# Norm boundaries of a two-layer encoder: sample tiles handled in pairs, another order on VectorE, two weight units split ahead

## The chip, the cores and the metric

The kernel runs on one core of one Trainium2 chip. The metric is the time of one execution on the device in microseconds (us). Five engines work side by side, each with its own in-order queue of instructions: TensorE (PE, with its weight loads shown apart as PEld), VectorE (DVE), ScalarE (ACT), GpSimd (POOL) and SyncE (SP), which here only issues transfers. An instruction that waits holds up everything behind it in its queue.

## The reference

Two sequences, a prompt of 512 tokens and a sample of 256 tokens, run through two layers of the same form. D is 1024.

```python
for l in range(DEPTH):                                   # 2 layers
    mod = (silu(c) @ ada_w[l] + ada_b[l]).reshape(B, 9, D)
    h = x * (1 + mod[:, 1]) + mod[:, 0]
    x = layer_norm(ALPHA*x + 0.5*(1 + mod[:, 2]) * swiglu(h, ffn1), ln[l, 0])
    h = x * (1 + mod[:, 4]) + mod[:, 3]
    o = concat(rms(window_attention(h)), rms(hyena(h))) @ w_out[l]
    x = layer_norm(ALPHA*x + (1 + mod[:, 5]) * o, ln[l, 1])
    h = x * (1 + mod[:, 7]) + mod[:, 6]
    x = layer_norm(ALPHA*x + 0.5*(1 + mod[:, 8]) * swiglu(h, ffn2), ln[l, 2])
```

There are six parts: feed-forward (FFN), mixer, FFN, and the same again. Between two parts stands a layer norm followed by the modulation of the next part. These five places are called boundaries 1 to 5 here. After boundaries 1 and 4 the next part is a mixer, after 2, 3 and 5 it is an FFN. Boundaries 2 and 5 come out of a mixer.

## The kernel before

Activations lie with features on the partitions: eight feature tiles d = 0 to 7 of 128 features, each with 512 prompt columns and 256 sample columns. Every product is done in three matmuls, since both operands are split in a high part (fp32r) and a low part (the rest): high weight by high activation, high weight by low activation, low weight by high activation (`mm3`). The low part of an activation is made by VectorE as value minus high part (`Norm.low`, L400), and the matmuls that read it wait for it.

Weights come in units of 128x1024 floats. `w_load` (L236) lets SP bring a unit into one of seven buffers slot_r; `w_ahead` (L243) then splits it into a buffer slot_w: ScalarE copies the high part, VectorE subtracts for the low part, and then the next load is asked for. `w_take` hands out split units in order. So a weight unit is ready when both engines have got to its split in their queues.

A boundary is written in `final` (L547). First `sample_out` makes the last product of the sample. Then a loop over d makes the prompt's last product (18 matmuls of 512 columns for each d out of an FFN, 12 out of a mixer). In that loop the sample's norm is worked off beside it: `stats` (sums over features by transposes and reductions), `bcast` (TensorE spreads 1/sigma and mean/sigma over the partitions, into two PSUM banks), and `apply` (L385) for two feature tiles per d. One `apply` is: VectorE multiplies by the first bank and subtracts the second (tile t), GpSimd writes the normed x, ScalarE writes the high part of the next h and its full value, and VectorE later subtracts for the low part. The last statement of each turn is `add` (L333): VectorE adds the product to x (scalar_tensor_tensor, called the residual here), ScalarE squares it, GpSimd adds it to the sum S, and VectorE adds the previous square to Q.

Then `Proj.head` (L459) starts the next part. It takes n units (4 before a mixer, 6 before an FFN) and makes for each the sample's product, 24 matmuls of 256 columns, in the order of the units; after unit 0 it calls the prompt's `stats`, and after the third unit `bcast` and eight prompt `apply`. Only then come the prompt's products, first for four units together and feature tile by feature tile, then for units 4 and 5. Before an FFN the full values of feature tiles 4 to 7 are kept in four of the seven slot_r (`Fast.full`, L689), and `Fast.early` (L701) takes two more for a later pair of units, after unit 0.

The order of the work is that of the program text; buffers are handed out by a rehearsal of the program, so that a tile gets the buffer that has been free longest. Each operation is recorded through one helper, L70, so rows below are told apart by tiles: slot_s holds activations, slot_w split weights, slot_r raw weights and full values, slot_t temporaries, bank a PSUM bank.

Of the kernel before, what the change touches and what calls it, by code (L numbers as in the profile page):

```python
# [14 lines left out]
ALU = mybir.AluOpType  # L15
AX = mybir.AxisListType

P = 128
D = 1024
ND = D // P  # L20
# [10 lines left out]
SEQ = (slice(0, LP), slice(LP, T), slice(0, LP // 2), slice(LP // 2, LP))  # L31
SLEN = (LP, LS, LP // 2, LP // 2)
# [45 lines left out]
class _Memory:  # L78
# [32 lines left out]
    def const(self, name, shape, dtype=F32):  # L111
        if not self.real:
            return _View(None)
        return self.pool.tile([P] + shape, dtype, tag=name, name=name)[:]
# [46 lines left out]
def _program(mem, nc, x_in, c_col, c_row, w_units, ada_nat, ada_t, ada_b, ln_p, conv_p, sink_in, grp_in,  # L161
             f_z, f_w1, f_v, f_w23, f_w4, f_decay, f_bias, f_t, dft_k, dft_y, dft_u, rope_in, mask_in, sgn_in, y_out):
    vec, act, gp, pe, sp = (mem.engine(getattr(nc, n) if mem.real else None)
                            for n in ("vector", "scalar", "gpsimd", "tensor", "sync"))
# [4 lines left out]
    def slot_w(shape, dtype=F32R):  # L169
        return mem.alloc("slot_w", shape, dtype)  # L170
# [6 lines left out]
    def slot_t(shape, dtype=F32):  # L177
        return mem.alloc("slot_t", shape, dtype)
# [9 lines left out]
    def f32(ap):  # L188
        return ap.bitcast(F32)

    def tt(out, a, b, op, eng=vec):
        eng.tensor_tensor(out=out, in0=a, in1=b, op=op)

    def ts(out, a, s1, s2=None, op0=ALU.mult, op1=ALU.add, eng=vec):
        if s2 is None:
            eng.tensor_scalar(out=out, in0=a, scalar1=s1, scalar2=None, op0=op0)
        else:
            eng.tensor_scalar(out=out, in0=a, scalar1=s1, scalar2=s2, op0=op0, op1=op1)
# [4 lines left out]
    def acopy(out, a):  # L203
        act.activation(out=out, in_=a, func=AF.Copy)

    def affine(out, a, scale, bias):
        act.activation(out=out, in_=a, func=AF.Identity, scale=scale, bias=bias)
# [11 lines left out]
    lnp = const("lnp", [DEPTH, 3, 2, ND])  # L219
# [12 lines left out]
    n_units = len(w_order)  # L232
    w_raw, w_split = {}, {}
    w_state = {"dma": 0, "split": 0, "next": 0, "limit": w_stops.pop(0), "raws": 3}

    def w_load(upto):  # L236
        while w_state["dma"] < min(upto, w_state["limit"]):
            i = w_state["dma"]
            w_raw[i] = slot_r([D])
            sp.dma_start(w_raw[i], w_units[w_order[i]])  # L240
            w_state["dma"] += 1

    def w_ahead(n):  # L243
        while w_state["split"] < min(w_state["next"] + n, w_state["limit"]):
            i = w_state["split"]
            w_load(i + 1)
            raw = w_raw.pop(i)
            w = slot_w([2, D])
            acopy(w[:, 0], raw)
            tt(w[:, 1], raw, f32(w[:, 0]), ALU.subtract)  # L250
            w_split[i] = w
            w_state["split"] += 1
            w_load(i + w_state["raws"])
# [27 lines left out]
    class Feat:  # L281
# [9 lines left out]
        def __call__(self, d, cols):  # L291
            if d // 4 not in self.t:
                self.more(d // 4)
            return self.t[d // 4][:, d % 4, cols]

    def new_h():
        return Feat(F32R), Feat(F32R)

# [20 lines left out]
    class Norm:  # L319
# [65 lines left out]
        def apply(self, s, d):  # L385

            n, c = SLEN[s], SEQ[s]
            x, t = self.x(d, c), slot_t([n])
            tt(t, x, self.r[s][:, :n], ALU.mult)
            if len(self.waiting) > 1:  # L390
                self.low()
            tt(t, t, self.mr[s][:, :n], ALU.subtract)
            ts(x, t, lnp[:, self.l, self.which, 0, d:d + 1], lnp[:, self.l, self.which, 1, d:d + 1], eng=gp)
            hh, hl, G, B = self.nxt
            v = t if self.full is None else self.full(d, c)
            affine(hh(d, c), t, G[:, d, s:s + 1], B[:, d, s:s + 1])
            affine(v, t, G[:, d, s:s + 1], B[:, d, s:s + 1])
            self.waiting.append((hl(d, c), hh(d, c), v))

        def low(self):  # L400
            if self.waiting:
                lo, hi, t = self.waiting.pop(0)
                tt(lo, t, f32(hi), ALU.subtract)
# [124 lines left out]
    def sample_out(os, norm):  # L528

        for o in os:  # L530
            for i in range(4):
                if i in o.hooks:
                    o.hooks[i]()
                outs = []
                for j in range(2):
                    b, more = o.place(1, 2 * i + j, j == 1)
                    o.d([(b, 1)], 2 * i + j, more=more)
                    outs.append(b)
                for j in range(2):
                    if o is os[-1]:  # L540
                        norm.add(2 * i + j, 1, outs[j])
                    else:
                        norm.plain(2 * i + j, 1, outs[j])
                pump(1)
        drain()

    def final(os, norm, proj, n_head, spill):  # L547

        sample_out(os, norm)
        o = os[-1]  # L550
        n_units = sum(o.n for o in os)
        when = (0, 2, 3) if n_units > 4 else (1, 3, 4)
        for d in range(ND):
            bp, more = o.place(0, d)
            for i, part in enumerate(os):
                part.d([(bp, 0)], d, more=more or i > 0, less=part is not o)
            w_ahead(min(4, 6 - n_units + sum((d + 1) * part.n // 8 for part in os)))
            if d == when[0]:
                norm.stats(1)
            if d == when[1]:  # L560
                norm.bcast(1)
            for i in range(2 * (d - when[2]), 2 * (d - when[2]) + 2):
                if 0 <= i < ND:
                    norm.apply(1, i)
            norm.add(d, 0, bp)
        for i in range(2 * (ND - when[2]), ND):
            norm.apply(1, i)
        for j in range(2):
            spill(1, j)
        norm.low()  # L570
        norm.low()
        norm.squares()
        w_ahead(6)

        def hook(i):
            if i == 0:
                norm.stats(0)
            elif i == 2:
                norm.bcast(0)
                for d in range(ND):  # L580
                    norm.apply(0, d)
                    if d % 4 == 3:
                        spill(0, d // 4)
                norm.low()
                norm.low()
            if i == 0:
                proj.early()

        proj.head(n_head, hook)
# [82 lines left out]
    class Fast:  # L672
# [144 lines left out]
        def late(self):  # L817

            j = self.j
            self.prep_a_high(j)  # L820
            self.prep_a_low(j)
            self.sums(j)
            for low in (self.prep_b(j), self.prep_c(j), self.prep_v3(j)):
                low()
            self.raw.pop(j)
# [302 lines left out]
    x = Feat()  # L1128
# [30 lines left out]
    G, B = modul(0, 0, None)  # L1159
    filt[0].spectra(1, sides(ts1[2], skip, ts1[3], skip, skip, filt[1].flush, skip, skip))  # L1160
    ts1[4]()
    ts1[5]()
    filt[1].flush()
    h = new_h()

    def first_h(d):
# [9 lines left out]
    part = swiglu(x, *h, 0, 0)  # L1176
# [578 lines left out]
    for i in range(len(PARTS)):  # L1755
# [5 lines left out]
        part = part[1](lambda os, xx, coef, i=i: finish(i, os, xx, coef))  # L1761
# [159 lines left out]
```

## Time and profile before

| what | value |
|---|---|
| median of 3 runs | 2927.01 us (2925.14 to 2927.79) |
| profiled execution, its own time | 2925.08 us |
| its span in the trace | 2923.3 us |
| TensorE busy | 2837.8 us (97%) |
| VectorE busy | 2138.7 us (73%) |
| ScalarE busy | 1345.9 us (46%) |
| GpSimd busy | 331.5 us (11%) |
| mean granted TensorE clock | 0.989 of full speed |

The span runs from the first to the last instruction. In rows of the timeline the columns are start, duration, engine, operation with tiles and shape, and in square brackets the idle time of the engine before it with what ended that idle time. A row with "x5" holds five instructions in sequence, and its duration covers all five.

### The profile page before, as it was taken

How to read it: one execution, taken by the hardware profiler on the slowest of the kernel's cores; microseconds unless marked ns; L12 is line 12 of the kernel's file. 1: busy time of each engine (PE TensorE's matmuls, PEld its weight loads, DVE VectorE, ACT ScalarE, POOL GpSimd, SP SyncE). 2: the span in 40 equal slices, each digit the busy share in tenths (PEclk: the TensorE clock that was granted, in tenths of full speed). 3: DMA queues.
4: the chain of work that ended last, by engine and by line, in shares of the span. 5: the costliest groups of instructions: out<-in, count | busy, mean ns of one | idle time of the engine just before them, and what ended most of it. 6: DMA issues, size and time to landing. Idle time of an engine off the chain costs nothing. (4 is left out here: it accounts for less than half of the span.)

```text
span 2923.3 us, 42304 instructions
## 1 busy us (share of the span) xinstructions
PE 2837.8 (97%) x16564; PEld 2599.3 (89%) x16564; DVE 2138.7 (73%) x3797; ACT 1345.9 (46%) x2307; POOL 331.5 (11%) x394
## 2 busy tenths in 40 slices
PE   9999999999999999999999999999999999999998
PEld 3789999988888889999988999998888888999997
DVE  5788778878968887786588777657896787444558
ACT  3544444444366544444445444444436654444444
POOL 2400000021000400000030000002100030000000
PEclk9999999999999999999999999999999999999999
DMA  5546665542121135664333665343312112455432
GB/s 203 194 174 173 189 176 163 145 147 102 68 73 61 55 134 155 194 195 120 107 120 123 180 175 159 104 111 133 107 70 74 60 50 92 82 115 116 99 108 82
DMA packets 102608, 364.67 MB, mean 125 GB/s; under 512 B 13750, under 2 KB 17031, under 8 KB 99208
## 3 DMA queue, kind: packets, MB, share of 16 engines
q1 hardware_dynamic: 74968, 259.88, 24.8%
q0 software_dynamic: 27440, 102.08, 16.3%
q8 instruction: 130, 2.13, 0.3%
q14 instruction: 70, 0.57, 0.1%
HBM read 284.33 MB, written 80.74 MB: 125 GB/s over the span
## 5 line engine op out<-in xcount | busy, mean ns | idle before, releaser
L70 PE MATMUL bank<-slot_s,slot_w 128*128 128x384 f32 (+2 forms) x13176 | 2321.4, 336 | 46.6 <-DVE slot_s L70 27.1
L70 PEld LDWEIGHTS bank<-slot_s,slot_w 128*128 128x128 f32 x13176 | 2129.7, 190 | 215.0 <-DVE slot_s L70 23.3
L70 DVE TENSOR_TENSOR slot_w<-slot_w,slot_w 128x1024 fp32r<-128x1024 f32 (+2 forms) x444 | 369.8, 864 | 4.1 <-ACT slot_w L70 1.6
L70 DVE CUSTOM_DVE_ANT_0 slot_t<-slot_r,slot_r 128x1024 bf16<-128x1024 f32 x256 | 311.5, 1223 | 78.5 <-DMA x_spill<-slot_t 49.0
L70 DVE TENSOR_TENSOR slot_w<-slot_r,slot_w 128x1024 fp32r<-128x1024 f32 (+1 forms) x194 | 222.1, 1153 | 114.6 <-ACT slot_w L70 113.2
L70 ACT ACTIVATE slot_w<-slot_w 128x1024 fp32r<-128x1024 f32 (+1 forms) x298 | 249.6, 838 | 118.5 <-DVE slot_w L70 118.5
L70 ACT ACTIVATE slot_t<-bank,tiny 128x512 f32<-128x512 f32 (+1 forms) x256 | 147.3, 580 | 307.0 <-PE bank L70 303.7
L70 POOL DMA_DIRECT2D x_spill<-slot_t x128 | 110.4, 862 | 1410.1 <-ACT slot_t L70 1410.1
L70 ACT ACTIVATE slot_w<-slot_r 128x1024 fp32r<-128x1024 f32 (+1 forms) x194 | 189.0, 992 | 155.3 <-DVE slot_r L70 96.8
L70 ACT ACTIVATE slot_t<-slot_t 128x384 f32<-128x384 f32 (+2 forms) x161 | 84.0, 526 | 332.8 <-DVE slot_t L70 332.6
L70 DVE TENSOR_TENSOR slot_t<-bank,slot_t 128x384 f32<-128x384 f32 x228 | 125.2, 554 | 145.6 <-PE bank L70 74.8
L70 DVE TENSOR_TENSOR slot_s<-slot_t,slot_s 128x768 fp32r<-128x768 f32 (+2 forms) x190 | 153.0, 809 | 51.9 <-ACT slot_s L70 47.6
L70 ACT ACTIVATE slot_t<-bank 128x384 f32<-128x384 f32 (+3 forms) x282 | 139.7, 496 | 104.0 <-PE bank L70 101.5
L70 ACT ACTIVATE slot_s<-slot_t 128x768 fp32r<-128x768 f32 (+2 forms) x160 | 113.8, 717 | 160.0 <-DVE slot_t L70 155.5
L70 PE MATMUL bank<-slot_s,slot_r 128*128 128x384 f32 x912 | 172.0, 337 | 0.0
L70 PEld LDWEIGHTS bank<-slot_s,slot_r 128*128 128x128 f32 x912 | 160.6, 188 | 0.0
L70 DVE TENSOR_TENSOR slot_r<-slot_w,slot_r 128x512 fp32r<-128x512 f32 x76 | 52.0, 684 | 105.0 <-ACT slot_r L70 104.8
L70 ACT ACTIVATE slot_t<-slot_s 128x256 f32<-128x256 f32 (+1 forms) x132 | 65.7, 509 | 109.8 <-DVE slot_s L70 101.3
L70 PE MATMUL bank<-slot_w,slot_s 128*128 128x256 f32 x864 | 107.8, 284 | 2.6 <-DVE slot_w L70 1.7
L70 PEld LDWEIGHTS bank<-slot_w,slot_s 128*128 128x128 f32 x864 | 104.7, 191 | 3.4 <-DVE slot_w L70 2.1
L70 DVE SCALAR_TENSOR_TENSOR slot_t<-bank,slot_t 128x384 f32<-128x384 f32 x76 | 42.3, 556 | 84.7 <-PE bank L70 83.4
L70 ACT ACTIVATE slot_s<-slot_t,tiny,tiny 128x256 fp32r<-128x256 f32 (+1 forms) x104 | 70.0, 703 | 54.6 <-DVE slot_t L70 54.6
(137 smaller groups left out, 2138.3 us busy)
## 6 DMA issues: line engine op xcount, KB each, us to landing
slot_r<-w_units SPq DMA_DIRECT2D x170, 512.0 KB, 4.9
slot_w<-w_units SPq DMA_DIRECT2D x146, 512.0 KB, 4.1
slot_r<-ada_t SPq DMA_DIRECT2D x128, 512.0 KB, 6.1
x_spill<-slot_t POOLq DMA_DIRECT2D x128, 384.0 KB, 5.3
slot_s<-x_spill POOLq DMA_DIRECT2D x12, 1536.0 KB, 8.1
x_spill<-slot_s POOLq DMA_DIRECT2D x10, 1024.0 KB, 4.6
slot_r<-ada_nat SPq DMA_DIRECT2D x16, 512.0 KB, 5.7
g_main<-slot_s POOLq DMA_DIRECT2D x4, 1536.0 KB, 10.1
```

Of the source, the lines that this page charges most:

```text
L70: return getattr(real, name)(*args, **kwargs)
```

## The change

In the loop of `final`, `apply` for two tiles is replaced by `apply2`: multiply and subtract run once over a pair of feature tiles (2 x 256 columns, the banks read twice by a broadcast), ScalarE writes both high parts and then both full values. Before a mixer the low parts of a pair are one instruction, before an FFN two. In each turn the order on VectorE is now: pair's multiply and subtract, the addition to Q, low parts of the pair before, residual. Weight units are split at most two ahead in the loop (up to four before), and two ahead at its end (six before). Before an FFN only two loads run ahead from the start of the loop (`raws`).

```diff
+    def beside(f, d, m, cols):
+        f(d, cols)
+        return f.t[d // 4][:, d % 4:d % 4 + m, cols]
+    def wide(b, m, n):
+        return b[:, :n].unsqueeze(1).to_broadcast([P, m, n])
...
+        def apply2(self, s, d):
+            n, c = SLEN[s], SEQ[s]
+            x, t = beside(self.x, d, 2, c), slot_t([2, n])
+            tt(t, x, wide(self.r[s], 2, n), ALU.mult)
+            tt(t, t, wide(self.mr[s], 2, n), ALU.subtract)
+            hh, hl, G, B = self.nxt
+            hi, lo = beside(hh, d, 2, c), beside(hl, d, 2, c)
+            for i in range(2):
+                affine(hi[:, i], t[:, i], G[:, d + i, s:s + 1], B[:, d + i, s:s + 1])
+            vs = []
+            for i in range(2):
+                ts(x[:, i], t[:, i], lnp[...], lnp[...], eng=gp)
+                vs.append(t[:, i] if self.full is None else self.full(d + i, c))
+                affine(vs[i], t[:, i], G[:, d + i, s:s + 1], B[:, d + i, s:s + 1])
+            if self.full is None:
+                self.waiting.append((lo, hi, t))
+            else:
+                for i in range(2):
+                    self.waiting.append((lo[:, i], hi[:, i], vs[i]))
+        def late(self, n):
+            while len(self.waiting) > n:
+                self.low()
...
         n_units = sum(o.n for o in os)
+        if norm.full is not None:
+            w_state["raws"] = 2
...
-            w_ahead(min(4, 6 - n_units + sum((d + 1) * part.n // 8 for part in os)))
+            w_ahead(min(2, 6 - n_units + sum((d + 1) * part.n // 8 for part in os)))
...
-            for i in range(2 * (d - when[2]), 2 * (d - when[2]) + 2):
-                if 0 <= i < ND:
-                    norm.apply(1, i)
+            was = len(norm.waiting)
+            if 0 <= d - when[2] < ND // 2:
+                norm.apply2(1, 2 * (d - when[2]))
+            norm.squares()
+            norm.late(len(norm.waiting) - was)
             norm.add(d, 0, bp)
-        for i in range(2 * (ND - when[2]), ND):
-            norm.apply(1, i)
+        for i in range(2 * (ND - when[2]), ND, 2):
+            norm.apply2(1, i)
+        norm.late(0)
         for j in range(2):
             spill(1, j)
-        norm.low()
-        norm.low()
         norm.squares()
-        w_ahead(6)
+        w_ahead(2)
```

VectorE at boundary 2, the last two turns of the loop, before: an `apply` writes t (slot_t from slot_s and a bank), a low part is slot_s from slot_s or slot_r and slot_s, the addition to Q is slot_t_3 on itself.

```order
L70 SCALAR_TENSOR_TENSOR slot_s6_1042_7774<-bank2_1245_8980,tiny9_1020_7668,slot_s6_1042_7774 128x512
L70 TENSOR_TENSOR slot_t3_1190_8602<-slot_t3_1190_8602,slot_t0_1244_8977 128x512
L70 TENSOR_TENSOR slot_t4_1249_9024<-slot_s6_1042_7774,bank4_1235_8936 128x256
L70 TENSOR_TENSOR slot_s9_1242_8968<-slot_s4_1240_8964,slot_s7_1241_8965 128x256
L70 TENSOR_TENSOR slot_t4_1249_9024<-slot_t4_1249_9024,bank5_1236_8939 128x256
L70 TENSOR_TENSOR slot_t5_1253_9034<-slot_s6_1042_7774,bank4_1235_8936 128x256
L70 TENSOR_TENSOR slot_s9_1242_8968<-slot_s4_1240_8964,slot_s7_1241_8965 128x256
L70 TENSOR_TENSOR slot_t5_1253_9034<-slot_t5_1253_9034,bank5_1236_8939 128x256
L70 SCALAR_TENSOR_TENSOR slot_s6_1042_7774<-bank6_1209_8734,tiny9_1020_7668,slot_s6_1042_7774 128x512
```

VectorE at the same place, changed:

```order
L70 SCALAR_TENSOR_TENSOR slot_s6_1038_7758<-bank6_1205_8718,tiny9_1016_7652,slot_s6_1038_7758 128x512
L70 TENSOR_TENSOR slot_t5_1245_9024<-slot_s6_1038_7758,bank4_1227_8910 128x512
L70 TENSOR_TENSOR slot_t5_1245_9024<-slot_t5_1245_9024,bank5_1228_8913 128x512
L70 TENSOR_TENSOR slot_t3_1186_8586<-slot_t3_1186_8586,slot_t0_1244_9009 128x512
L70 TENSOR_TENSOR slot_s0_1241_8996<-slot_r5_1242_9000,slot_s2_1240_8995 128x256
L70 TENSOR_TENSOR slot_s0_1241_8996<-slot_r2_1243_9003,slot_s2_1240_8995 128x256
L70 SCALAR_TENSOR_TENSOR slot_s6_1038_7758<-bank3_1209_8744,tiny9_1016_7652,slot_s6_1038_7758 128x512
L70 TENSOR_TENSOR slot_s0_1241_8996<-slot_r4_1246_9030,slot_s2_1240_8995 128x256
L70 TENSOR_TENSOR slot_s0_1241_8996<-slot_r1_1247_9033,slot_s2_1240_8995 128x256
L70 TENSOR_TENSOR slot_t3_1186_8586<-slot_t3_1186_8586,slot_t1_1248_9039 128x512
```

The four 256-column operations on banks have become two of 512 columns right behind the residual, the addition to Q and the low parts stand behind them, and the last two low parts directly follow the last residual.

VectorE at the start of the head of boundary 3, before: splits of weight units (slot_w from slot_r), the prompt's `stats` (TENSOR_REDUCE to tiny), the first `apply`.

```order
L70 TENSOR_TENSOR slot_w1_1812_13699<-slot_r0_1794_13600,slot_w1_1812_13699 128x1024
L70 TENSOR_TENSOR slot_w3_1813_13702<-slot_r4_1796_13605,slot_w3_1813_13702 128x1024
L70 TENSOR_REDUCE tiny11_1817_13740<-bank5_1815_13730 128x4
L70 TENSOR_REDUCE tiny11_1817_13740<-bank2_1816_13735 128x4
L70 TENSOR_SCALAR tiny11_1817_13740<-tiny11_1817_13740 128x4
L70 TENSOR_TENSOR tiny11_1817_13740<-tiny11_1817_13740 128x4
L70 SCALAR_TENSOR_TENSOR tiny11_1817_13740<-tiny11_1817_13740 128x4
L70 TENSOR_SCALAR tiny11_1817_13740<-tiny11_1817_13740 128x4
L70 TENSOR_TENSOR slot_t2_1820_13777<-slot_t2_1820_13777,bank4_1814_13705 128x256
L70 TENSOR_TENSOR slot_s4_1821_13779<-slot_t2_1820_13777,slot_s4_1821_13779 128x256
L70 TENSOR_TENSOR slot_t3_1825_13818<-slot_s9_1740_13176,bank3_1823_13808 128x512
```

VectorE at the same place, changed, from the split of unit 2 to the first `apply`:

```order
L70 TENSOR_TENSOR slot_w2_1796_13648<-slot_r0_1768_13458,slot_w2_1796_13648 128x1024
L70 TENSOR_REDUCE tiny11_1800_13687<-bank5_1798_13677 128x4
L70 TENSOR_REDUCE tiny11_1800_13687<-bank2_1799_13682 128x4
L70 TENSOR_SCALAR tiny11_1800_13687<-tiny11_1800_13687 128x4
L70 TENSOR_TENSOR tiny11_1800_13687<-tiny11_1800_13687 128x4
L70 SCALAR_TENSOR_TENSOR tiny11_1800_13687<-tiny11_1800_13687 128x4
L70 TENSOR_SCALAR tiny11_1800_13687<-tiny11_1800_13687 128x4
L70 TENSOR_TENSOR slot_w0_1803_13700<-slot_r2_1797_13651,slot_w0_1803_13700 128x1024
L70 TENSOR_TENSOR slot_t1_1805_13729<-slot_t1_1805_13729,bank4_1795_13647 128x256
L70 TENSOR_TENSOR slot_s9_1806_13731<-slot_t1_1805_13729,slot_s9_1806_13731 128x256
L70 TENSOR_TENSOR slot_w1_1808_13736<-slot_r2_1804_13703,slot_w1_1808_13736 128x1024
L70 TENSOR_TENSOR slot_t3_1812_13775<-slot_s7_1732_13148,bank3_1810_13765 128x512
```

Before, all six units were split when the head began. Now units 3 and 4 (slot_w0_1803, slot_w1_1808) are split behind `stats`, and the raw data of unit 4 goes into the buffer slot_r2 that unit 3's raw data had. The same engine at the end of the eight prompt `apply`, changed:

```order
L70 TENSOR_TENSOR slot_s2_1784_13565<-slot_r1_1786_13572,slot_s0_1783_13564 128x512
L70 TENSOR_TENSOR slot_t0_1819_13823<-slot_t0_1819_13823,bank1_1811_13770 128x512
L70 TENSOR_TENSOR slot_s2_1784_13565<-slot_r3_1790_13606,slot_s0_1783_13564 128x512
L70 TENSOR_TENSOR slot_s2_1784_13565<-slot_r5_1791_13609,slot_s0_1783_13564 128x512
L70 TENSOR_TENSOR slot_w3_1820_13833<-slot_r2_1809_13739,slot_w3_1820_13833 128x1024
L70 TENSOR_TENSOR slot_t4_1821_13860<-slot_t4_1821_13860,bank0_1807_13735 128x256
```

TensorE at the same boundary, changed, where the sample's product of unit 5 begins (its weights are slot_w3_1820):

```order
L70 MATMUL bank6_1822_13865<-slot_s0_1783_13564,slot_w1_1808_13736 128x256
L70 MATMUL bank6_1822_13865<-slot_s3_1774_13493,slot_w3_1820_13833 128x256
L70 MATMUL bank6_1822_13865<-slot_s1_1775_13494,slot_w3_1820_13833 128x256
L70 MATMUL bank6_1822_13865<-slot_s3_1774_13493,slot_w3_1820_13833 128x256 x2
L70 MATMUL bank6_1822_13865<-slot_s1_1775_13494,slot_w3_1820_13833 128x256
```

The split of unit 5 stands behind the last low part of the eight prompt `apply` on VectorE, while on TensorE the unit's sample product stands directly behind unit 4's and ahead of the prompt's products, as before. Boundaries 2 and 5 have the same order in their heads. Before a mixer the head has four units, and the splits that stand behind the `apply` are of units used after the head.

## Rows read from the trace of the kernel before

**Rows 1.** The page, busy time, share of the span, instructions.
```profile
PE 2837.8 (97%) x16564; PEld 2599.3 (89%) x16564; DVE 2138.7 (73%) x3797; ACT 1345.9 (46%) x2307; POOL 331.5 (11%) x394
```

**Rows 2.** TensorE's waits, boundaries 2 and 5: total us, times, longest.
```profile
PE bank L70 <- DVE slot_s L70: 5.9, 5, 2.4
...
PE bank L70 <- DVE slot_s L70: 5.2, 4, 2.4
```

**Rows 3.** Timeline of TensorE at boundaries 1, 3 and 4.
```profile
652.38 0.86 PE L70 MATMUL bank<-slot_s,slot_w 128*128 128x256 f32 x5 [2.06 <-DVE slot_s L70]
...
1520.58 0.86 PE L70 MATMUL bank<-slot_s,slot_w 128*128 128x256 f32 x5 [1.05 <-DVE slot_s L70]
...
2042.89 0.86 PE L70 MATMUL bank<-slot_s,slot_w 128*128 128x256 f32 x5 [2.15 <-DVE slot_s L70]
```

**Rows 4.** Stretches behind waits: length, busy by engine, clock (before the last two columns), DMA.
```profile
653.30:656.60 3.30, 3.30 (x18) 3.30 (x17) 3.30 (x4) 0.00 (x0) 0.32 (x1) 0.50 0.93 271
997.25:1001.50 4.25, 4.25 (x20) 4.25 (x21) 4.25 (x6) 0.81 (x1) 1.23 (x2) 0.50 0.72 217
2382.27:2384.27 2.00, 2.00 (x6) 1.43 (x6) 2.00 (x6) 1.69 (x4) 1.39 (x2) 0.50 0.00 0
2386.27:2390.65 4.38, 4.38 (x20) 4.38 (x21) 4.38 (x7) 0.82 (x1) 1.25 (x2) 0.50 0.74 222
2042.90:2047.30 4.40, 4.40 (x37) 4.40 (x38) 4.40 (x7) 0.21 (x1) 1.22 (x2) 1.00 0.75 220
```

**Rows 5.** Timeline of VectorE and GpSimd, one turn at boundary 2.
```profile
987.31 1.60 POOL L70 TENSOR_TENSOR slot_t<-slot_t,slot_s 128x512 f32<-128x512 f32 x1
...
987.69 0.41 DVE L70 TENSOR_TENSOR slot_t<-slot_s,bank 128x256 f32<-128x256 f32 x1
988.02 1.17 DVE L70 TENSOR_TENSOR slot_s<-slot_s,slot_s 128x256 fp32r<-128x256 f32 x1
...
989.78 0.41 DVE L70 TENSOR_TENSOR slot_s<-slot_s,slot_s 128x256 fp32r<-128x256 f32 x1
...
990.44 0.74 DVE L70 SCALAR_TENSOR_TENSOR slot_s<-bank,tiny,slot_s 128x512 f32<-128x512 f32 x1
...
991.11 0.68 DVE L70 TENSOR_TENSOR slot_t<-slot_t,slot_t 128x512 f32<-128x512 f32 x1
...
991.71 0.41 DVE L70 TENSOR_TENSOR slot_t<-slot_s,bank 128x256 f32<-128x256 f32 x1
```

**Rows 6.** Timeline of TensorE, head of boundary 3.
```profile
1521.28 1.03 PE L70 MATMUL bank<-ident,slot_t 128*128 128x128 f32 x8
1522.07 6.00 PE L70 MATMUL bank<-slot_s,slot_w 128*128 128x256 f32 x48
...
1528.70 21.60 PE L70 MATMUL bank<-slot_s,slot_w 128*128 128x256 f32 x128
```

**Rows 7.** Timeline of VectorE and ScalarE, head of boundary 3.
```profile
1521.38 2.35 DVE L70 TENSOR_TENSOR slot_w<-slot_r,slot_w 128x1024 fp32r<-128x1024 f32 x2
...
1523.65 1.27 DVE L70 TENSOR_REDUCE tiny<-bank 128x4 f32<-128x512 f32 x2
...
1525.43 0.17 DVE L70 TENSOR_SCALAR tiny<-tiny 128x4 f32<-128x4 f32 x1
...
1528.54 0.69 DVE L70 TENSOR_TENSOR slot_t<-slot_s,bank 128x512 f32<-128x512 f32 x1 [1.48 <-PE bank L70]
...
1544.58 0.80 ACT L70 ACTIVATE slot_r<-slot_t,tiny,tiny 128x512 f32<-128x512 f32 x1
...
1545.41 0.69 DVE L70 TENSOR_TENSOR slot_s<-slot_r,slot_s 128x512 fp32r<-128x512 f32 x1 [0.99 <-ACT slot_r L70]
```

**Rows 8.** Split on ScalarE at boundary 3, timeline.
```profile
1518.71 1.99 ACT L70 ACTIVATE slot_w<-slot_r 128x1024 fp32r<-128x1024 f32 x2
```

**Rows 9.** DMA issues: round boundary 2, then the whole page: count, KB, us to landing.
```profile
slot_r<-w_units SPq DMA_DIRECT2D x9, 512.0 KB, 4.0
...
slot_r<-ada_t SPq DMA_DIRECT2D x128, 512.0 KB, 6.1
```

More of the change, by code (lines that the diff above doesn't have):

```diff
@@ L398, in apply @@
             self.waiting.append((hl(d, c), hh(d, c), v))
+        def apply2(self, s, d):
[9 more added lines that the diff above has]
+            for i in range(2):
+                ts(x[:, i], t[:, i], lnp[:, self.l, self.which, 0, d + i:d + i + 1],
+                   lnp[:, self.l, self.which, 1, d + i:d + i + 1], eng=gp)
+                vs.append(t[:, i] if self.full is None else self.full(d + i, c))
[8 more added lines that the diff above has]
+                self.low()
         def low(self):
```

## The prediction

> **What bounds the kernel now.** I read the page first: TensorE is busy for 97% of the span [rows 1], so a change elsewhere counts only by what it adds to or takes from TensorE's idle time. Next come TensorE's waits in the stretches that the change touches. At boundary 2 it waits five times, 5.9 us in all, and at boundary 5 four times, 5.2 us, each time for a low part that VectorE writes into slot_s [rows 2]. The timeline shows one such wait at each of the others: 2.06, 1.05 and 2.15 us at boundaries 1, 3 and 4 [rows 3]. The sum is 16.4 us.
>
> The stretches behind these waits show a second price. After the waits at boundaries 1, 2 and 5 TensorE works at a granted clock of 0.50, its lower level of 1.2 GHz, for 3.30, 4.25 and 2.00 + 4.38 us, while after the 2.15 us at boundary 4 it stays at 1.00 [rows 4]. Work at half clock takes twice as long, so half of these stretches is lost: 1.7, 2.1 and 3.2 us. All that better low parts could give back is therefore 16.4 + 7.0 = 23.4 us.
>
> Why VectorE is late is seen in one turn of the loop at boundary 2. GpSimd's sum runs from 987.31 to 988.91. Beside it VectorE's operation on a bank takes 0.41 us as always, but the low part that follows takes 1.17 and ends 0.28 us behind the sum; the next low part, with no sum beside it, takes 0.41 [rows 5]. So one low part in each turn loses 0.76 us.
>
> **The change part by part: the loop.** A pair's multiply and subtract are 2 instructions instead of 4. A 512-column one from a bank takes 0.69 [rows 7], against 2 x 0.41 [rows 5]. These 1.4 us fill most of the sum's 1.6 us, and the low parts come behind it. A turn of VectorE out of a mixer is then 1.4 for the pair, 0.60 for the addition to Q and 0.67 for the residual (start to start), and two low parts of some 0.33 each: 3.3 us. Its length before is 991.71 - 987.69 = 4.0 [rows 5]. TensorE needs for a turn 12 matmuls of 512 columns; the 128 matmuls of the head are 72 of 256 columns at 6.00/48 = 0.125, and 56 of 512, which leaves 0.225 each [rows 6], so 2.7 us. VectorE still falls behind by about 0.5 us in each of three turns. Then the last residual ends 2.2 us after TensorE's last prompt product, and the low parts of tiles 6 and 7 follow when GpSimd's last sum begins: tile 6 at 2.5, tile 7, behind the sum, at about 4.1. TensorE's unit 0 wants them after 2.4 and 2.9 us. I leave 1.6 us of waiting at boundaries 2 and 5, between 0.4 (no low part is held by the sum) and the whole 5.9.
>
> The Trainium skill bears on this, in "SBUF — State Buffer", section "Who interferes with whom": a VectorE instruction with two inputs in SBUF contends with a GpSimd instruction that reads SBUF, and whichever comes second stands still until the other is done; with one SBUF input there is no contention. The rows agree (1.17 against 0.41). It speaks against the last pair of the change, which stands right where a sum begins: by the rule both low parts may wait, 1.9 us at each of the two boundaries, and without it 0.4, so 3.8 against 0.8 in the sum.
>
> Out of an FFN a turn of TensorE is 18 matmuls, 4.1 us, longer than VectorE's 3.3, and the last pair's low parts stand ahead of the last residual. There I expect the waits to go, with the half clock of boundary 1. The gains are: boundary 1, 2.06 + 1.7; boundary 3, 1.05; boundary 4, 2.15; boundary 2, 5.9 + 2.1 - 1.6; boundary 5, 5.2 + 3.2 - 1.6. That is 20.2 us, between 7 (boundaries 2 and 5 unchanged) and 23.4.
>
> **The change part by part: the weight units.** Splitting two ahead removes no split, it moves them. Of six units of a head before an FFN, three are now split in the head, and their place in VectorE's and ScalarE's queues decides. The split of unit 5 is behind all eight prompt `apply`, yet TensorE's sample product of unit 5 comes ahead of all prompt products. TensorE's queue is in order, so it stands still there. Before, every unit was split when the head began; this work (ScalarE 1.99/2 = 1.0 and VectorE 2.35/2 = 1.2 for each unit [rows 7, 8]) was hidden beside prompt products.
>
> I work this out at boundary 3, from E, the end of unit 0's sample product (1521.2, when the transposes of `stats` follow [rows 6]). Before, TensorE has units 1 and 2 done and `bcast` made at 1528.70, E + 7.5, and three sample units of 24 x 0.125 = 3.0 bring the first prompt product to E + 16.5.
>
> With the change VectorE does `stats` after the transposes: from 1523.65 to 1525.60 is 1.95 [rows 7], so E + 1.1 to E + 3.1. The split of unit 3 follows, to E + 4.3. Only then is its raw buffer free for unit 4: four of seven slot_r hold full values, two hold the raw pair loaded early, and one is left. SP issues the load; transfers of this size and kind landed in 4.0 us there [rows 9], so E + 8.4. ScalarE's copy and VectorE's subtraction follow, E + 9.4 and E + 10.6, just in time for TensorE's unit 4 (E + 10.5). The eight `apply` are queued behind this split. Before, they run from 1528.54 to 1546.10, 17.56 us, and ScalarE's last full value ends at 1545.38, 16.84 us after the start [rows 7]; so they end at E + 28.2, and ScalarE's at E + 27.4. ScalarE copies unit 5's high part by E + 28.4, and VectorE has its low part at E + 29.7.
>
> TensorE is ready for unit 5 at E + 13.5. Two matmuls can go at E + 28.4, the third needs the low weights at E + 29.7, and 22 more take 2.75. After such a wait I count the clock as after those of boundaries 2 and 5, half for some 4.3 us of work time [rows 4], of which 3.0 fall on matmuls: 1.5 more. Unit 5 ends at E + 34.0 instead of E + 16.5, a loss of 17.5 us. Nothing takes it back: the prompt products run 23 us longer than anything queued for VectorE behind them needs. It happens at boundaries 2, 3 and 5, since 1 and 4 have four units in the head, all split ahead of the `apply`.
>
> Bounds of this loss, from the same rows: if the load of unit 4 has landed in time, the `apply` start at E + 7.3 as before (1528.54), 3.3 less; at full clock 1.5 less; so 12.7 at the least. If the load takes 6.1 us, as the same size does elsewhere [rows 9], 2.1 more, with a little more at half clock 20. I take 17.5, since the load of rows 9 is from such a boundary.
>
> **The sum.** 3 x 17.5 = 52.5 lost, 20.2 gained: 32.3 us slower. The profiled execution took 2925.08 (span 2923.3), which gives 2957.4; the median of the three runs is 1.9 us above it, and I give the time on the median, 2927.01 + 32.3 = 2959.
>
> **The rivals.** (1) Faster: unit 5 is ready in time, and only the loop's gain is seen, 2927.0 - 20.2 = 2907. For it speaks that the waits of rows 2 and 3 are real and their cause is treated. For unit 5 to be in time at E + 13.5, the `apply` block, starting at E + 7.3 at the earliest and followed by 2.2 us of split, would have to last 4 us; from there on the sign of the whole would turn at about 6.7 us of loss for each boundary, a block of some 9 us. It lasted 17.56. (2) Slower, but less: the load of unit 4 is no link of the chain; 3 x 14.2 - 20.2 = 22.4, so 2949. For it: the split of unit 3 may come earlier than I place it. Against it: the buffer is the same one, slot_r2, for units 3, 4 and 5. (3) Slower by more: the pairs bring nothing out of a mixer, since the low parts of the last pair meet the last sum; 52.5 - 7.0 = 45.5, so 2972. For it: the 1.17 us of rows 5. Against it: TensorE waited in four or five places there, and only the last pair is in that position. (4) No change: loss and gain cancel, which needs a loss of 6.7 us at each FFN boundary; no row gives so short a block.
>
> **How the numbers follow.** Chances: the forecast 0.58, rival 2 0.18, rival 3 0.15, rival 4 0.04, rival 1 0.05. The range of the first three, with the bounds above (3 x 12.7 - 23.4 = 15 to 3 x 20 - 7 = 53), is narrowed at both ends to 2946 and 2976, which I expect to hold 8 in 10. Within 0.2% (5.9 us) is what a measurement of this kernel can't tell from no change; slower by more has the first three cases, 0.91, no change 0.04, faster 0.05.
>
> **What would show it.** In the changed kernel's trace TensorE should show, at boundaries 2, 3 and 5, one wait of 13 to 16 us for ScalarE's slot_w in front of 256-column matmuls, followed by a short one for VectorE's slot_w and a stretch at clock 0.50. VectorE's first prompt `apply` should start some 3 us later after the transposes than before, with ScalarE waiting for a load slot_r<-w_units in front of it. The waits for VectorE's slot_s at boundaries 1, 3 and 4 should be gone, and at 2 and 5 shrink to one or two of under 2 us in all. The loss is wrong if TensorE's sample product of unit 5 starts without a wait, or if the `apply` block is much shorter than 17 us; the gain is wrong if low parts still take over 1 us in the loop.

## The result, and the profile after

The changed kernel takes 2949.8 us (2949.1 to 2953.7), the kernel before beside it 2927.4: a ratio of 1.0081 [1.0069, 1.0093] (95% interval in brackets), 22.4 us slower. The forecast was 32 us slower, 2959, with a range of 2946 to 2976. The profiled run of the changed kernel took 2949.14 us, its span is 2947.3, 24.0 us longer than before.

TensorE's busy time, the first figure of this row of the page, is 4.7 us shorter than before [rows 1], so the loss is idle time.

```profile
PE 2833.1 (96%) x16564; PEld 2595.8 (88%) x16564; DVE 2131.1 (72%) x3749; ACT 1346.7 (46%) x2307; POOL 336.6 (11%) x394
```

TensorE's waits over the whole span (total us, times, longest) say for what. ScalarE's slot_w is the high part of a weight unit.

```profile
PE bank L70 <- ACT slot_w L70: 45.3, 7, 14.8
PE bank L70 <- DVE slot_s L70: 20.0, 17, 4.5
...
PE bank L70 <- ACT slot_t L70: 7.5, 7, 3.2
```

The timeline of TensorE shows the places. The first three rows are the ends of unit 0 at boundary 2, where the last low parts are late (2.11 us in three waits, against 5.9 in five before [rows 2]; at boundary 5 they are 2.15, against 5.2). The others are unit 5 at boundaries 2, 3 and 5: two matmuls after the high part, the rest after the low part. Behind the stall 262 matmuls run without a wait, past the end of the head.

```profile
985.11 0.98 PE L70 MATMUL bank<-slot_s,slot_w 128*128 128x256 f32 x6 [0.89 <-DVE slot_s L70]
986.51 0.63 PE L70 MATMUL bank<-slot_s,slot_w 128*128 128x256 f32 x3 [0.43 <-DVE slot_s L70]
987.93 0.50 PE L70 MATMUL bank<-slot_s,slot_w 128*128 128x256 f32 x2 [0.79 <-DVE slot_s L70]
...
1016.39 0.79 PE L70 MATMUL bank<-slot_s,slot_w 128*128 128x256 f32 x2 [14.70 <-ACT slot_w L70]
1017.65 53.60 PE L70 MATMUL bank<-slot_s,slot_w 128*128 128x256 f32 x262 [0.47 <-DVE slot_w L70]
...
1551.60 0.80 PE L70 MATMUL bank<-slot_s,slot_w 128*128 128x256 f32 x2 [14.35 <-ACT slot_w L70]
...
2426.74 0.80 PE L70 MATMUL bank<-slot_s,slot_w 128*128 128x256 f32 x2 [14.78 <-ACT slot_w L70]
2428.00 54.85 PE L70 MATMUL bank<-slot_s,slot_w 128*128 128x256 f32 x262 [0.47 <-DVE slot_w L70]
```

The waits of 2.06, 1.05 and 2.15 us at boundaries 1, 3 and 4 [rows 3] have no row any more. The clock (before the last two columns) is half behind each stall, and full behind boundary 1's former wait and the small ones of boundary 2, where it was half before [rows 4]:

```profile
1016.39:1020.30 3.91, 3.44 (x14) 3.15 (x15) 1.96 (x3) 0.63 (x2) 0.00 (x0) 0.50 0.90 303
1551.60:1556.10 4.50, 4.04 (x17) 3.74 (x18) 1.96 (x3) 0.64 (x2) 0.00 (x0) 0.50 0.92 320
2426.74:2433.40 6.66, 6.19 (x26) 5.80 (x27) 1.96 (x3) 0.85 (x3) 0.00 (x0) 0.50 0.42 160
988.28:992.50 4.22, 4.22 (x38) 4.22 (x37) 4.12 (x9) 1.97 (x3) 1.73 (x3) 1.00 0.82 245
...
649.17:652.50 3.33, 3.33 (x31) 3.33 (x30) 3.23 (x9) 0.65 (x1) 1.26 (x3) 1.00 0.72 221
```

The chain to the stall at boundary 3, from E = 1523.84. VectorE: the split of unit 3, of unit 4 (3.04 us late, for ScalarE's copy), the first `apply`, the last low part, the split of unit 5.

```profile
1526.83 1.23 DVE L70 TENSOR_TENSOR slot_w<-slot_r,slot_w 128x1024 fp32r<-128x1024 f32 x1
...
1532.65 1.23 DVE L70 TENSOR_TENSOR slot_w<-slot_r,slot_w 128x1024 fp32r<-128x1024 f32 x1 [3.04 <-ACT slot_w L70]
1533.79 0.68 DVE L70 TENSOR_TENSOR slot_t<-slot_s,bank 128x512 f32<-128x512 f32 x1
...
1550.63 0.69 DVE L70 TENSOR_TENSOR slot_s<-slot_r,slot_s 128x512 fp32r<-128x512 f32 x1 [0.98 <-ACT slot_r L70]
1551.58 1.23 DVE L70 TENSOR_TENSOR slot_w<-slot_r,slot_w 128x1024 fp32r<-128x1024 f32 x1 [0.25 <-ACT slot_w L70]
```

ScalarE's copies of units 4 and 5: the first waits for the load.

```profile
1531.55 1.06 ACT L70 ACTIVATE slot_w<-slot_r 128x1024 fp32r<-128x1024 f32 x1 [2.40 <-DMA slot_r<-w_units]
...
1550.51 1.04 ACT L70 ACTIVATE slot_w<-slot_r 128x1024 fp32r<-128x1024 f32 x1
```

One turn of VectorE at boundary 2, from one residual to the next and the last low parts. It takes 985.31 - 981.98 = 3.33 us, 4.0 before [rows 5]; two low parts take 0.74 behind the addition to Q, and 1.91 where GpSimd's last sum (986.20 to 987.60) runs beside them.

```profile
981.98 0.74 DVE L70 SCALAR_TENSOR_TENSOR slot_s<-bank,tiny,slot_s 128x512 f32<-128x512 f32 x1
982.64 0.67 DVE L70 TENSOR_TENSOR slot_t<-slot_s,bank 128x512 f32<-128x512 f32 x1
983.35 0.69 DVE L70 TENSOR_TENSOR slot_t<-slot_t,bank 128x512 f32<-128x512 f32 x1
983.96 0.76 DVE L70 TENSOR_TENSOR slot_t<-slot_t,slot_t 128x512 f32<-128x512 f32 x1
984.64 0.74 DVE L70 TENSOR_TENSOR slot_s<-slot_r,slot_s 128x256 fp32r<-128x256 f32 x2
985.31 0.74 DVE L70 SCALAR_TENSOR_TENSOR slot_s<-bank,tiny,slot_s 128x512 f32<-128x512 f32 x1
985.97 1.91 DVE L70 TENSOR_TENSOR slot_s<-slot_r,slot_s 128x256 fp32r<-128x256 f32 x2
```

To see where the 24.0 us arose, I divided every trace at two marks of TensorE at each boundary: the four transposes of the sample's `stats` (in the loop) and the eight of the prompt's (in the head, at E). The five stretches between them, called loop stages here, are 35.14 + 27.98 + 33.70 + 34.74 + 27.98 = 159.5 us before and 32.83 + 23.05 + 32.79 + 32.83 + 23.05 = 144.6 after. So everything up to E became 15.0 us shorter, and the rest of the span 39.0 longer. From E to the next mark the change costs 13.7, 15.9 and 13.0 us after boundaries 2, 3 and 5 (here to the end of the span), and saves 1.4 and 0.7 after 1 and 4; the start of the program, which the change does not touch, was 1.6 shorter. Each stage comes from one profiled execution. The loop stages repeat well: four kernels with the same loop and splits in it (changed, e3, e4, e5) have 144.6. The rest repeats less well: its first stretch, ahead of boundary 1, which no kernel here changes, lies between 616.0 and 619.6, so differences of 2 or 3 us in the rest can't be put down to an edit. Below, times are medians, and each comparison is with the kernel before on the same chip (2927.9 for e1 to e4, 2927.2 for e5 to e8).

| kernel | time | span | loop stages | rest of the span |
|---|---|---|---|---|
| before | 2927.9 | 2923.3 | 159.5 | 2763.8 |
| changed | 2949.8 | 2947.3 | 144.6 | 2802.7 |
| e1, loop alone | 2921.5 | 2917.0 | 156.1 | 2760.9 |
| e2, splits alone | 2956.3 | 2952.0 | 151.1 | 2800.9 |
| e3, unit 5 ahead | 2923.2 | 2920.5 | 144.6 | 2775.9 |
| e4, loads ahead | 2943.2 | 2941.3 | 144.6 | 2796.7 |
| e5, both ahead | 2916.5 | 2914.8 | 144.6 | 2770.2 |
| e6, pairs, old order | 2919.9 | 2916.6 | 152.6 | 2764.0 |
| e7, old loop | 2922.6 | 2919.6 | 151.0 | 2768.6 |
| e8, last sum moved | 2909.9 | 2908.0 | 142.9 | 2765.1 |

### The profile page after: what moved, and what is told of

Same layout as the page of the kernel before. It is cut to its first block, busy times and chain, and to the rows that moved or that the text cites. A ratio compares the mean times of both kernels' runs of the same rounds, so it can differ in the third digit from the quotient of the medians.

```text
span 2947.3 us, 42204 instructions
## 1 busy us (share of the span) xinstructions
PE 2833.1 (96%) x16564; PEld 2595.8 (88%) x16564; DVE 2131.1 (72%) x3749; ACT 1346.7 (46%) x2307; POOL 336.6 (11%) x394
## 4 chain that ended last, share of the span: by engine, by line
PE 77%; DVE 13%; ACT 5%; DMA 3%; issue 2%; SPq 0%; POOL 0%; DVEq 0%; ACTq 0%; POOLq 0%
PE bank L70 77%; DVE slot_t L70 5%; DVE slot_w L70 3%; DVE slot_s L70 3%; ACT slot_w L70 2%; DVE slot_r L70 2%; DMA slot_r<-w_units 1%; ACT slot_s L70 1%; DMA slot_r<-ada_t 1%; DVE tiny L70 1%; ACT slot_t L70 1%; ACT slot_r L70 0%; DMA g_samp<-slot_w 0%; SPq L70 0%; DMA tiny<-ada_b 0%
## 5 line engine op out<-in xcount | busy, mean ns | idle before, releaser
L70 DVE TENSOR_TENSOR slot_s<-slot_t,slot_s 128x768 fp32r<-128x768 f32 (+2 forms) x182 | 146.9, 811 | 51.8 <-ACT slot_s L70 47.6
L70 DVE SCALAR_TENSOR_TENSOR slot_s<-bank,tiny,slot_s 128x256 f32<-128x256 f32 (+1 forms) x160 | 87.1, 564 | 17.3 <-PE bank L70 17.1
```

What stands on the lines that cost most here:

```text
L70: return getattr(real, name)(*args, **kwargs)
```

## The experiments

**Which part gains, which loses (e1, e2).** e1 is the changed kernel with the old splits:

```diff
-        if norm.full is not None:
-            w_state["raws"] = 2
...
-            w_ahead(min(2, 6 - n_units + sum(...)))
+            w_ahead(min(4, 6 - n_units + sum(...)))
...
-        w_ahead(2)
+        w_ahead(6)
```

> The changed loop (pairs, order on VectorE), with the weight units split as before: up to four ahead in the loop, six at its end, three raw loads ahead. Theory A (the loop gains, the splits lose): the three stalls of 14.4 to 14.8 us in front of unit 5 are gone, the waits for slot_s at boundaries 1, 3 and 4 stay away and about 2.1 us are left at boundaries 2 and 5; the change lost 14.3 + 15.8 + 14.4 = 44.4 us at the three FFN boundaries, so this kernel takes 2949.8 - 44.4 = 2905, some 20 us less than before. The waits of 1.7 to 2.0 us at the end of the three FFN heads, gone in the changed kernel, should be back. Theory B (the loop gains because fewer splits stand in it, not by pairs and order): with the splits back the waits for slot_s come back, and the time is within 6 us of before, 2921 to 2927.

e2 is the kernel before with the opposite edit.

> The loop as before, with only the weight units split at most two ahead and two raw loads ahead. Theory A: stalls of about 14.5 us in front of unit 5's sample product at boundaries 2, 3 and 5, the waits for slot_s as before (5.9 and 5.2 us, 2.06, 1.05, 2.15), and the waits at the end of the FFN heads gone: 2927.4 + 44.4 = 2972. Theory B: the waits for slot_s shrink here although the loop is old, and the time is 2950 to 2957. The prediction on record without anything given back: 2927.4 + 52.5 = 2980.

e1: ratio 0.9981 [0.9972, 0.999], 6.4 us faster. e2: 1.0102 [1.0088, 1.0115], 28.4 us slower. Together 22.0, the whole change. Both times lie where Theory B had them, and Theory A fell, though the two numbers of the prediction had summed to nearly the right total: the new loop earns 6.4 us, not 20, and the splits cost 28, not 44 to 52. In the timeline of TensorE of e1 a wait for GpSimd's sum S (slot_t) has taken the place of the one at boundary 1 (and at 3 and 4), boundary 2 waits 4.3 us again, and the wait at the end of the head is back:

```profile
650.91 1.21 PE L70 MATMUL bank<-ident,slot_t 128*128 128x128 f32 x8 [1.21 <-POOL slot_t L70]
...
986.33 1.20 PE L70 MATMUL bank<-slot_s,slot_w 128*128 128x256 f32 x6 [1.79 <-DVE slot_s L70]
989.63 2.43 PE L70 MATMUL bank<-slot_s,slot_w 128*128 128x256 f32 x9 [2.10 <-DVE slot_s L70]
992.47 0.80 PE L70 MATMUL bank<-slot_s,slot_w 128*128 128x256 f32 x2 [0.41 <-DVE slot_s L70]
1050.18 13.20 PE L70 MATMUL bank<-slot_s,slot_w 128*128 128x384 f32 x72 [2.08 <-ACT slot_t L70]
```

VectorE of e1 shows what a split in the loop costs: its own 1.23 us, and 1.65 of waiting for ScalarE's copy, ahead of the residuals and low parts that are queued behind it.

```profile
975.35 1.23 DVE L70 TENSOR_TENSOR slot_w<-slot_r,slot_w 128x1024 fp32r<-128x1024 f32 x1 [1.65 <-ACT slot_w L70]
```

In e2, with the old loop, moving the splits out leaves 0.60 of the 2.06 us at boundary 1, 4.0 of 5.9 at boundary 2, and 0.64 of the 2.15 at boundary 4; the loop stages are 8.5 us shorter. The new loop shortens them by 3.4 with the old splits. So most of the 15.0 came from the edit that the prediction had put down as pure loss. The 3.1 us that the two edits gain in the loop only together don't show in the sum of 22.0: behind the loops the changed kernel loses 39.0 us, e2 loses 37.1 and e1 gains 2.9. Of the 4.8 us between, 2.7 are longer stalls (13.14 to 14.46 us in e2, 14.35 to 14.78 in the changed kernel).

```profile
650.02 0.86 PE L70 MATMUL bank<-slot_s,slot_w 128*128 128x256 f32 x5 [0.60 <-DVE slot_s L70]
...
1019.49 0.80 PE L70 MATMUL bank<-slot_s,slot_w 128*128 128x256 f32 x2 [13.56 <-ACT slot_w L70]
```

**What unit 5 waits for (e3, e4).** e3, in the head of the changed kernel:

```diff
-                    w_ahead(min(2, 6 - len(ws)))
+                    w_ahead(min(3, 6 - len(ws)))
```

> The changed kernel with one number changed: in the head a unit is split up to three ahead instead of two, so unit 5's split stands ahead of the eight prompt apply and unit 4's behind stats. Theory A (the apply block is what unit 5 waits for): the stall in front of unit 5 falls from 14.4 to 14.8 us to 2 to 4 us (two loads of 4 us and two splits in a row after unit 3). The apply block then starts some 6 us later than in the changed kernel, and since what VectorE has queued behind it (mixed, late) moves with it while TensorE's prompt products start earlier, a wait of 4 to 8 us should appear at the end of each FFN head: 2949.8 - 3 x 12 + 3 x 6 = 2932, between 2920 and 2940. Rival (the loads of units 4 and 5 in one buffer are the price, not the block): the stall stays above 8 us, and the time above 2940.

e4, in `final` of the changed kernel:

```diff
-        if norm.full is not None:
-            w_state["raws"] = 2
...
-            if i == 0:
+            if i == 2:
                 proj.early()
```

> The changed kernel with three raw loads ahead and the early pair of raw loads asked for behind the prompt apply instead of behind stats, so that unit 4's load is asked for a unit earlier; unit 5's split stays behind the apply. Theory A: VectorE's first prompt apply starts 2.5 to 3 us earlier (E + 7.3 as before instead of E + 10), the stall in front of unit 5 is 11.5 to 12 us instead of 14.4 to 14.8, and the time 2949.8 - 3 x 2.8 = 2941. Rival 2 of the prediction (the load of unit 4 is no link of the chain): no change, 2950.

e3 took 2923.2 us, 0.9986 [0.9978, 0.9995]: one number takes away all three stalls and 27 us. The stall is wholly gone (2 to 4 us were expected), and in its place TensorE waits at the end of the head for the weights of the next stage and for ScalarE's copy of a bank into slot_t:

```profile
1567.27 0.61 PE L70 MATMUL bank<-slot_s,slot_w 128*128 128x384 f32 x2 [1.12 <-ACT slot_w L70]
1568.53 4.09 PE L70 MATMUL bank<-slot_s,slot_w 128*128 128x384 f32 x22 [0.65 <-DVE slot_w L70]
1576.99 14.35 PE L70 MATMUL bank<-slot_s,slot_w 128*128 128x384 f32 x72 [4.37 <-ACT slot_t L70]
```

e4 took 2943.2, 1.0057 [1.0045, 1.007], where Theory A had 2941 and the prediction's rival 2 no change. VectorE's first `apply` starts 7.4 us behind E (1523.78) instead of 10.0, and the stall is 11.87 instead of 14.35. The load of unit 4 is a link of the chain, of 2.5 to 2.9 us at each of the three boundaries.

```profile
1530.08 1.23 DVE L70 TENSOR_TENSOR slot_w<-slot_r,slot_w 128x1024 fp32r<-128x1024 f32 x1 [0.53 <-ACT slot_w L70]
1531.22 0.68 DVE L70 TENSOR_TENSOR slot_t<-slot_s,bank 128x512 f32<-128x512 f32 x1
```

```profile
1549.05 0.79 PE L70 MATMUL bank<-slot_s,slot_w 128*128 128x256 f32 x2 [11.87 <-ACT slot_w L70]
```

**The loop without the stall (e5, e6, e7).** e5 is e3 and e4 together.

> Three raw loads ahead, the early pair asked for behind the prompt apply (as e4), and units split up to three ahead in the head (as e3); the rest is the changed kernel. What the runs so far say: with the splits out of the loop the loop stage of the five boundaries is 15.0 us shorter than before (159.5 to 144.6, from the transposes of the sample's stats to those of the prompt's), and half clock at boundary 1 is 1.4 less; with the loads ahead and unit 5's split ahead of the apply block there is no stall in front of unit 5, and the block starts about 1.2 us later than before, so that the waits at the end of the FFN heads are 3 us instead of 2. Sum: 2927.9 - 16.4 + 3 x 1.2 = 2915, between 2911 and 2919. Rival (the loads still hold the block up as in e3): 2923.

e6 is e5 with VectorE's old order: in `apply2` the waiting low parts come between multiply and subtract.

```diff
             tt(t, x, wide(self.r[s], 2, n), ALU.mult)
+            self.late(0)
             tt(t, t, wide(self.mr[s], 2, n), ALU.subtract)
...
-            norm.squares()
-            norm.late(len(norm.waiting) - was)
             norm.add(d, 0, bp)
```

> As e5, with the pairs of tiles but VectorE's old order in the loop: residual, addition to Q, pair's multiply, low parts of the pair before, subtract. If the order is what gains (low parts out of GpSimd's sum: 3.33 us for a turn at boundary 2 against 4.04), the turn is back at 4.0 us and the time is that of the old loop with the same splits (e7), 6 to 7 us above e5, 2921. If the pairs gain (2 instructions of 0.6 start to start for 4 of 0.33), it is that of e5, 2915.

e7 is the kernel before with the splits and loads of e5.

> The loop as before (no pairs, old order), with the splits and loads of e5. The new loop alone shortened the loop stages by 3.4 us with the old splits, and by 15.0 - 8.5 = 6.5 us with the splits moved out: so 6.5 us above e5, 2921. Theory A (the pairs and the order earn most of the 20 us of the prediction) would have 14 to 20 us above e5, 2930 to 2935.

e5 took 2916.5, 0.9965 [0.9952, 0.9977]; e7 2922.6, 0.9986 [0.9977, 0.9995]: with the same splits the new loop is worth 6.1 us, as the loop stages say (151.0 against 144.6, 6.4 us). e6 took 2919.9, 0.9978 [0.9969, 0.9986], between the two, so its time doesn't decide between order and pairs, but its loop stages do: 152.6, no shorter than with the old loop. VectorE's turn in e6 is 983.56 - 979.37 = 4.19 us, and its two low parts, beside the sum again, take 1.80:

```profile
979.37 0.74 DVE L70 SCALAR_TENSOR_TENSOR slot_s<-bank,tiny,slot_s 128x512 f32<-128x512 f32 x1
...
981.24 1.80 DVE L70 TENSOR_TENSOR slot_s<-slot_s,slot_s 128x256 fp32r<-128x256 f32 x2
...
983.56 0.73 DVE L70 SCALAR_TENSOR_TENSOR slot_s<-bank,tiny,slot_s 128x512 f32<-128x512 f32 x1
```

The order shortens the loop stages; the pairs alone don't. The new order without pairs was not run. That e6 is nevertheless some 4.6 us faster than e7 behind the loops (2764.0 against 2768.6) is seen at the ends of the FFN heads: e6 waits 2.15, 3.08 and 2.16 us there and e7 3.09, 3.08 and 3.43, and the 72 matmuls behind the waits take 13.2 us each in e6, at full clock, and 15.55, 14.35 and 15.41 in e7, partly at half clock. Together that is 7.9 us; e6 gives 2.9 of them back to half clock at the start of the heads of boundaries 2 and 5. e5 has half clock at the ends too, so the 8.0 us of loop stages between e6 and e5 are only 3.4 in the time.

What e5 still loses lies at the end of the FFN heads: 3.25, 4.14 and 3.46 us of waiting, each followed by half clock (granted 0.50).

```profile
1045.59 15.46 PE L70 MATMUL bank<-slot_s,slot_w 128*128 128x384 f32 x72 [3.25 <-ACT slot_t L70]
...
1571.38 15.38 PE L70 MATMUL bank<-slot_s,slot_w 128*128 128x384 f32 x72 [4.14 <-ACT slot_t L70]
```

**The last sum (e8).** e8 is e5, with the prompt's last addition to S on VectorE behind the last low parts:

```diff
-                tt(self.S[:, c], self.S[:, c], x, ALU.add, eng=vec if s else gp)
+                if s or d < ND - 1:
+                    tt(self.S[:, c], self.S[:, c], x, ALU.add, eng=vec if s else gp)
...
         norm.late(0)
+        c = SEQ[0]
+        tt(norm.S[:, c], norm.S[:, c], norm.x(ND - 1, c), ALU.add)
```

> As e5, and the prompt's last addition to S is made by VectorE behind the last low parts instead of by GpSimd beside them. If the last two low parts take 1.91 us in the changed kernel (for 0.75 elsewhere) because GpSimd's sum runs beside them, they take 0.75 here, TensorE's three waits at boundaries 2 and 5 fall from 2.1 to about 1 us at each, and the time is 2 us below e5, 2913. If the sum is not what holds them, the waits stay at 2.1 and the time is that of e5 or, with the addition in VectorE's queue, up to 2 us above.

It took 2909.9, 0.9947 [0.9935, 0.996], the fastest kernel here, faster than both the one before and the changed one. Of VectorE's rows the first is the last pair of low parts in e8, which took 1.92 in e5:

```profile
985.99 0.82 DVE L70 TENSOR_TENSOR slot_s<-slot_r,slot_s 128x256 fp32r<-128x256 f32 x2
986.74 0.68 DVE L70 TENSOR_TENSOR slot_t<-slot_t,slot_s 128x512 f32<-128x512 f32 x1
```

So the sum is what held them. TensorE's waits at boundary 2 fall to 0.91 + 0.43 us, and the loop stages by 1.7. The other 4.9 us of the difference between the two medians are not shown to come from it: 2.1 of them lie ahead of boundary 1 in the two traces, the 72 matmuls behind the waits at the ends of the FFN heads have less half clock in e8 (14.12 to 14.34 us for 15.38 to 15.46), and the intervals of e5 and e8 overlap.

## Why the prediction was right, and where it was wrong

The direction and the mechanism of the loss were right. Unit 5's split stands behind the `apply` block and TensorE stands still for it: 14.35 to 14.8 us for the high part and 0.47 for the low part, where 14.9 and a short second wait were forecast. At boundary 3 the `apply` start at E + 10.0 (forecast E + 10.6), unit 5's high part is there at E + 27.7 (E + 28.4) and its low part at E + 29.0 (E + 29.7). The load was a link of the chain, as taken; e4 shows its price. Rival 2, whose number (2949) came out, is therefore wrong as a mechanism: the right time came from other terms. Rival 1's 2907 needed unit 5 in time; e3 and e5, where it is, give 2923 and 2916. Rival 3 had the waits at boundaries 2 and 5 stay; they fell from 5.9 and 5.2 us to 2.11 and 2.15.

Two steps failed. The first is "Nothing takes it back". The reason given, that the prompt products run longer than anything queued for VectorE, overlooked that TensorE had been waiting at the end of these heads for ScalarE's copy of a bank, which follows VectorE's work (at boundary 2 the copy runs from 1054.52 to 1054.99, and TensorE goes on at 1055.04): 1.7, 2.0 and 2.0 us in the kernel before, the last with some half clock behind it.

```profile
1055.04 13.19 PE L70 MATMUL bank<-slot_s,slot_w 128*128 128x384 f32 x72 [1.70 <-ACT slot_t L70]
...
1576.41 13.21 PE L70 MATMUL bank<-slot_s,slot_w 128*128 128x384 f32 x72 [1.97 <-ACT slot_t L70]
...
2444.17 14.33 PE L70 MATMUL bank<-slot_s,slot_w 128*128 128x384 f32 x72 [2.04 <-ACT slot_t L70]
```

The stall shifts TensorE's prompt products back against VectorE's work behind the `apply`, and in the changed kernel none of these waits has a row. e1 has them again (2.08, 2.00 and 2.05 us). e5, which takes the stall away, has more: at boundary 3 its `apply` start 2.0 us later than in e1 (E + 9.4 for E + 7.4), and at boundaries 2 and 5 TensorE, at full clock from E on, gets to the end of the head earlier. The 5.7 us of before, with the half clock and less 1.2 us of a wait behind them that grew at boundary 3 (from 0.40 to 1.55), are the larger part of the 8 to 10 us by which the forecast was too high. Another 1.6 us in the traces are the start of the program, which the change does not touch; the rest is not accounted for.

The second is the attribution. "Splitting two ahead removes no split, it moves them" counted what the splits cost where they go and nothing where they leave. They leave the loop, where each delayed residuals and low parts. Three quarters of the shortening that the prediction put down to pairs and order belong to this or to both edits together: 15.0 us of loop stages, of which the new loop alone gives 3.4, the splits alone 8.5, and the remaining 3.1 need both. The total hardly shows that, because the same term was merely credited to the wrong edit: these 15.0 us, and 4.4 of half clock that is gone behind E at boundaries 1, 2 and 5 (the transposes and 48 matmuls there take 6.6 us instead of 8.0 to 8.2), make 19.4, where 20.2 was forecast. Only e1 and e2 show it. Of the pairs themselves the prediction had the arithmetic without drawing the conclusion: 0.60 to 0.67 start to start for one 512-column operation and 0.33 for one of 256 are the same per column. What shortened the turn from 4.0 to 3.33 us is that the low parts left the sum (4.19 in e6, where they are beside it).

Of the smaller terms, the waits left at boundaries 2 and 5 were 2.1 instead of 1.6 each, and the half clock behind the stalls took (3.44 + 4.04 + 6.19) / 2 = 6.8 us instead of 4.5. With the waits of 43.8 and 1.4 us that makes 52.1 at the three stalls, where 52.5 was forecast; that the shorter waits and the longer half clock cancel is luck. The rows of boundary 1 and 2 at full clock agree with the forecast that the half clock there leaves with the waits. On the last pair the rule of the Trainium skill ("SBUF — State Buffer", "Who interferes with whom") agrees with e5 and e8: 1.92 us beside GpSimd's sum, 0.82 without. By that rule, taken for both low parts, the waits were to be 1.9, and they were 2.1. Here, too, terms cancel: e8, in which the sum holds no low part, still waits 1.34 and 1.35 us at boundaries 2 and 5, where the prediction had 0.4, so the sum costs some 0.8 us at each, one low part and not two.

## What to carry to other kernels

A split, load or copy that is moved has two prices: what it delays in the new place, and what it stops delaying in the old one; price both, and test the halves of a mixed change alone before crediting the sum to either. Ahead of a block of some 17 us on an in-order engine, look for the one instruction behind it that another engine needs first: here one number (three units ahead instead of two) moved it ahead of the block and was worth 27 us. A stall is partly paid back where the stalled engine would have had to wait later anyway, so look at the next wait behind it before summing.

## What the runs showed that was not expected

The length of a wait alone does not tell whether the lower clock follows. At the end of the head of boundary 5 TensorE waited 2.04 us before and 2.05 us in e1, at the same place and after the same work of some 50 us. The first windows row is of the kernel before, part of it at the lower level of 1.2 GHz (0.67 on the mean); the second is of e1, all of it at 2.4 GHz.

```profile
2444.17:2447.60 3.43, 3.43 (x14) 3.42 (x15) 2.32 (x4) 2.08 (x4) 0.00 (x0) 0.67 0.00 0
```

```profile
2439.19:2442.60 3.41, 3.41 (x20) 3.41 (x21) 2.30 (x4) 2.21 (x4) 0.00 (x0) 1.00 0.01 2
```

e6 and e7 show the same at a longer wait. At the end of the head of boundary 3 TensorE waits 3.08 us in both; behind it the granted clock is 1.00 in e6 (1572.24 to 1577.00, first row) and 0.51 in e7 (1574.56 to 1578.00, second row).

```profile
1572.24 13.22 PE L70 MATMUL bank<-slot_s,slot_w 128*128 128x384 f32 x72 [3.08 <-ACT slot_t L70]
```

```profile
1574.56 14.35 PE L70 MATMUL bank<-slot_s,slot_w 128*128 128x384 f32 x72 [3.08 <-ACT slot_t L70]
```

So a half-clock term behind a wait of this size may or may not come, and no run here shows what decides it: the prediction counted it as certain where the trace before had it.
